# A third raw weight place and an early start of the last branch products in a hybrid decoder trunk

## The chip, the cores and the metric

The kernel runs on one core of a Trainium2 chip. Its time is the device time of one execution in microseconds (us), the median of the runs. The engines are named as in the profile: PE multiplies matrices (PEld is the loading of its stationary operand), DVE and ACT do the work on vectors, POOL does a little of it, and SP issues nearly all the transfers between HBM and the on-chip memory. SP takes its instructions in the order in which they stand in its queue, and each waits there until what it reads or overwrites is ready; every other engine's queue works in the same way. PE accumulates into PSUM, of which the kernel uses banks of 128 x 512 numbers.

## The reference

One sequence of 512 positions, 1024 channels, two layers. A layer is a half-step feed-forward block, a mixing block and a second feed-forward block, each behind a norm and ahead of another. The mixing block is where most of the change lies (cut):

```
u = _rmsnorm(h, mix_pre_g[l]);  proj = u @ w_in[l]          # q, k, v of both causal branches, f_logit, q_mem
...
z = q k^T / 8                                               # stick-breaking branch, 8 heads of 64
w = exp(log_beta + log_between)  where key < query
...
z = q k^T / 8 + c[:, None] - c[None, :]                     # forgetting branch, 8 heads of 64; c = cumsum(log_f)
p = softmax(z  where key <= query)
...
merged = (g_sb * (o_sb @ w_br_sb[l]) + g_fx * (o_fx @ w_br_fox[l]) + g_mem * (o_mem @ w_br_mem[l]))
h = h + _rmsnorm(merged @ w_out[l], mix_post_g[l])          # g_* = sigmoid(u @ w_gate[l] + b_gate[l])
```

The memory branch has 4 heads of 128 over 256 memory positions. The feed-forward blocks are SwiGLU with a hidden width of 2816.

## The kernel before, in words

**Products and weights.** Every float32 product of weights is computed as three PE products of rounded halves: high by high, high by low, low by high (`mm3`, L210, L211, L212; one "product" of 128 x 512 outputs over 1024 inputs is thus 24 matmuls). So each weight is split: a `Unit` (some 512 KB) is fetched by SP into a *raw* place (`fetch`, L254), ACT writes the high half `wh` (L180, L183), DVE subtracts it from the raw values and writes the low half `wl` (L181, L184). There are two raw places and four each for `wh` and `wl`. When a unit has been split, `loaded` gives its raw place up and calls `Q.fetch_ahead()`, which issues the next fetches in the program as long as places are free by its count. A tile also waits at run time until the reads of the one that held its place before are done. Activations are split in the same way (`split`, L180 and L181): names such as `k`, `ptf`, `pts`, `o`, `ms` in the profile.

**Mixing.** Projections give q and k for pairs of heads (products `pq`, `pk`, units `raw_q`, `raw_k`). A head then is a chain that goes through the engines:

- a stick-breaking head (`zs`, `pts`, `pvs` and `ss` in the profile) has scores on PE, sigmoids on ACT and a scan on DVE; ACT sorts the 32-bit words into two 16-bit planes (`turn_out`), SP transposes the planes in a DMA (`turn_over`, L1146, tiles `ts`), ACT puts the words together again, the result is split into `pts`, and PE multiplies it by the values (`attend`, L1170);
- a forgetting head (`zf`, `ptf`, `pvf`, `sf`) adds, for each of four row blocks, the causal mask (L1241), q·k (L1251) and a product with the cumulated forget gates (L1252; its operand `qk` is written by POOL and DVE in `fox_pre`, L1229 to L1232). DVE takes the maximum (L1254), ACT the exponential (L1256), DVE scales (L1257, L1258). Then come planes and transposes as above; DVE joins the words (`joined`, L1156), the split gives `ptf`, PE multiplies by the values (L1170), and `sf` (L1173, L1174) and its split give the branch output `o`.

While a chain is on its way, PE works on gate products (`pg`: u by `w_gate`), branch products (`pb`: `o` by `w_br`, in `merge`) and the projections of the next heads.

**What sets the order.** A planner, `Queue`, writes the program. Jobs (a product with its units) stand in a list; `step` emits the next matmuls and loads four units ahead (`AHEAD`). `weave` runs the causal heads as chains beside the jobs: a chain yields ("pe", time) or ("wait", time), the time being counted in emitted PE work (a column of a matmul counts 1/2370 us), and while it waits, jobs are emitted, up to a `limit` on the list of jobs that belongs to the head. For a forgetting head the waits are `W_FX0` = 2.0 (scores to `turn_out`), `W_FX1` = 6.0 (to `joined`) and `W_FX2` = 5.2 (to `attend`, during which the next head's scores are begun). So a larger wait in the planner means that more matmuls are written before the head's next step; how long anything really takes is not known to it. The heads come as four pairs of each kind, the forgetting pairs in the order 2, 3, 0, 1 (`FOX`).

**The end of mixing.** The gates of the forgetting branch are computed ahead and saved (`gsave`). After the last head, `run` in `merge` reloads two gates (`gb`, L1470), forms two products `pb` over the four pairs of `o`, multiplies by the gate (L1483), adds to `merged` (`mg`, L1484), and splits to `ms`; this is done four times for 8 outputs. Then come the products of `w_out` (`pwo`), which read all eight `ms`.

**Places.** Beside raw, a tag `tri` has two places. They hold split words (`ptf`, `pts`, `pt` of memory heads), the joined words of heads before the split (`pw...`), the normed memory, and hidden rows in the feed-forward blocks.

## Time and profile before

| | before |
|---|---|
| median of 3 runs | 2352.35 us (2349.74 to 2352.86) |
| the profiled execution's own time | 2350.35 us |
| its span | 2348.5 us |
| PE busy | 2311.8 us (98%), 11239 matmuls |
| DVE busy | 1801.2 us (77%) |
| ACT busy | 1600.4 us (68%) |
| transfers | 380.11 MB, mean 162 GB/s |

The span is the part of an execution that the records cover; the times of rows are microseconds from its start. A row of a group reads: line, engine, operation, output<-inputs, count, busy time, mean time of one, and behind the last bar the idle time just before them on their engine, with what ended it. In a row of the timeline the idle time of the engine before it and its releaser stand in square brackets. A row of the waits names the waiting engine with its tile, what released it, and then the idle time, the number of waits and the longest. Tiles of different layers and numbers are shown under one name in the profile (`pvf` for all forgetting heads), so a place in the program is found by its time: the mixing block of layer 0 lies near 373 to 800 us up to `w_out`, that of layer 1 near 1560 to 1965 us.

### The profile page before, as it was taken

The page shows a single profiled execution, that of the slowest core. Times are in us where ns is not written, and L with a number is a line of the kernel's source. Part 1 is how long each engine was busy: PE and PEld are TensorE (multiplying, and loading weights), DVE is VectorE, ACT ScalarE, POOL GpSimd, SP SyncE. Part 2 cuts the span into 40 slices and gives each one's busy share as a digit, 9 for nine tenths or more (in the row PEclk, how much of TensorE's full clock was granted, in tenths as well). Part 3 has the DMA queues.
Part 4 walks back from the last instruction along what each step waited for, and adds up shares of the span by engine and source line. Part 5 has one row for each costly group of instructions (what it writes and reads, how often), then busy time and mean ns, then how long its engine had stood idle before and what let it go on. Part 6 is the DMA issues. An engine that isn't in the chain of part 4 may idle for free. (4 is left out here: it accounts for less than half of the span.)

```text
span 2348.5 us, 30426 instructions
## 1 busy us (share of the span) xinstructions
PE 2311.8 (98%) x11239; PEld 1941.7 (83%) x11239; DVE 1801.2 (77%) x2291; ACT 1600.4 (68%) x2286; POOL 89.7 (4%) x182
## 2 busy tenths in 40 slices
PE   9999999999999999999999999999999999999998
PEld 7888888878788788888898888888887888888887
DVE  8877876666787688878798778766667877887785
ACT  6677466878877556775556775668788685667744
POOL 0000000000111000000000000000011100000000
PEclk9999999999999999999999999999999999999999
DMA  6667455544445654674746665555444455566744
GB/s 206 194 175 221 144 194 149 122 103 116 114 115 125 213 189 155 188 203 147 230 138 190 193 188 167 191 140 118 117 101 124 110 162 193 169 186 177 221 137 148
DMA packets 399736, 380.11 MB, mean 162 GB/s; under 512 B 180170, under 2 KB 291042, under 8 KB 399588
## 3 DMA queue, kind: packets, MB, share of 16 engines
q1 hardware_dynamic: 399492, 378.15, 55.5%
q8 instruction: 88, 1.44, 0.3%
q14 instruction: 60, 0.49, 0.1%
q0 software_dynamic: 96, 0.03, 0.0%
HBM read 319.39 MB, written 16.78 MB: 143 GB/s over the span
## 5 line engine op out<-in xcount | busy, mean ns | idle before, releaser
L210 PE MATMUL pg<-us_a,wh_wg 128*128 128x512 f32 x384 | 153.7, 400 | 8.1 <-DVE k L181 8.1
L211 PE MATMUL pg<-us_a,wh_wg 128*128 128x512 f32 x384 | 152.8, 398 | 0.0
L212 PE MATMUL pg<-us_a,wl_wg 128*128 128x512 f32 x384 | 152.5, 397 | 0.0
L181 DVE TENSOR_TENSOR wl_dc<-raw_dc,wh_dc 128x1024 fp32r<-128x1024 f32 x50 | 61.0, 1223 | 44.7 <-ACT wh_dc L180 44.7
L181 DVE TENSOR_TENSOR wl_da<-raw_da,wh_da 128x1024 fp32r<-128x1024 f32 x50 | 60.8, 1223 | 44.4 <-ACT wh_da L180 44.3
L210 PEld LDWEIGHTS pg<-us_a,wh_wg 128*128 128x128 f32 x384 | 74.2, 193 | 24.2 <-issue 8.9
L211 PE MATMUL pda<-wl_da,aha 128*128 128x512 f32 x224 | 87.7, 392 | 0.0
L211 PE MATMUL pdc<-wl_dc,ahc 128*128 128x512 f32 x224 | 87.6, 391 | 0.0
L212 PEld LDWEIGHTS pg<-us_a,wl_wg 128*128 128x128 f32 x384 | 74.1, 193 | 16.1
L212 PE MATMUL pda<-wh_da,ala 128*128 128x512 f32 x224 | 87.2, 389 | 0.0
L212 PE MATMUL pdc<-wh_dc,alc 128*128 128x512 f32 x224 | 87.2, 389 | 0.0
L210 PE MATMUL pda<-wh_da,aha 128*128 128x512 f32 x224 | 86.6, 390 | 0.5 <-ACT pda L893 0.5
L211 PEld LDWEIGHTS pg<-us_a,wh_wg 128*128 128x128 f32 x384 | 74.3, 194 | 15.4
L210 PE MATMUL pdc<-wh_dc,ahc 128*128 128x512 f32 x224 | 86.5, 389 | 0.0
L180 ACT CAST wh_dc<-raw_dc 128x1024 fp32r<-128x1024 f32 x50 | 52.3, 1049 | 47.8 <-DMA raw_dc<-in_ffn_w_down_dram 14.9
L180 ACT CAST wh_da<-raw_da 128x1024 fp32r<-128x1024 f32 x50 | 52.1, 1050 | 45.5 <-DMA raw_da<-in_ffn_w_down_dram 13.9
L184 DVE SCALAR_TENSOR_TENSOR wl_wg<-raw_wg,wh_wg 128x1024 fp32r<-128x1024 f32 x48 | 58.5, 1222 | 24.5 <-ACT wh_wg L183 24.4
L180 ACT CAST wh_uc<-raw_uc 128x1024 fp32r<-128x1024 f32 x44 | 46.4, 1053 | 34.5 <-PE pwc1g L212 8.2
L180 ACT CAST wh_ua<-raw_ua 128x1024 fp32r<-128x1024 f32 x44 | 46.2, 1052 | 30.1 <-PE pwa0g L212 8.0
L181 DVE TENSOR_TENSOR wl_uc<-raw_uc,wh_uc 128x1024 fp32r<-128x1024 f32 x44 | 53.7, 1221 | 14.9 <-ACT wh_uc L180 14.9
L181 DVE TENSOR_TENSOR wl_gc<-raw_gc,wh_gc 128x1024 fp32r<-128x1024 f32 x40 | 48.5, 1221 | 19.6 <-ACT wh_gc L180 19.6
L181 DVE TENSOR_TENSOR wl_ga<-raw_ga,wh_ga 128x1024 fp32r<-128x1024 f32 x40 | 48.5, 1221 | 19.5 <-ACT wh_ga L180 19.5
(645 smaller groups left out, 8028.3 us busy)
## 6 DMA issues: line engine op xcount, KB each, us to landing
raw_da<-in_ffn_w_down_dram SPq DMA_DIRECT2D x66, 512.0 KB, 5.0
raw_dc<-in_ffn_w_down_dram SPq DMA_DIRECT2D x66, 512.0 KB, 4.5
raw_ga<-in_ffn_w_gate_dram SPq DMA_DIRECT2D x52, 512.0 KB, 4.9
raw_ua<-in_ffn_w_up_dram SPq DMA_DIRECT2D x52, 512.0 KB, 4.4
raw_gc<-in_ffn_w_gate_dram SPq DMA_DIRECT2D x52, 512.0 KB, 4.0
raw_uc<-in_ffn_w_up_dram SPq DMA_DIRECT2D x52, 512.0 KB, 4.3
raw_wg<-in_w_gate_dram SPq DMA_DIRECT2D x48, 512.0 KB, 3.7
raw_wo<-in_w_out_dram SPq DMA_DIRECT2D x24, 512.0 KB, 3.8
```

Source lines behind the costliest of these rows:

```text
L180: both = [nc.scalar.copy(h_ap, src)]
L181: make = lambda: nc.vector.tensor_tensor(l_ap, src, h_ap.bitcast(F32), ALU.subtract)
L184: make = lambda: nc.vector.scalar_tensor_tensor(l_ap, src, scale, h_ap.bitcast(F32), ALU.mult, ALU.subtract)
L210: nc.tensor.matmul(pt, lh, rh, start=start, stop=False, skip_group_check=free)
L211: nc.tensor.matmul(pt, lh, rl, start=False, stop=False, skip_group_check=free)
L212: nc.tensor.matmul(pt, ll, rh, start=False, stop=stop, skip_group_check=free)
```

## The change

1. **Places.** `tri` has one place instead of two, a new tag `word` has one, and raw has three instead of two. What stood in the two `tri` places is now divided: split words in `tri`, joined words of causal heads in `word`; hidden rows, first weights of a block, normed memory and the words of memory heads take one of each in turn.
2. **Forgetting heads.** The four q·k products are written ahead of the four products with `qk`. The planner's wait `W_FX0` is longer by a `slack` of 4.0 for the first forgetting head of each layer, and `W_FX1` is 6.5 instead of 6.0.
3. **The last branch products.** For the first two pairs of outputs of the forgetting branch (`dp` 0 and 1) the products over three of the four pairs of `o` (`FOX[:-1]`) become a job of their own (`part`), in banks that are kept: those of `dp` 0 in the tag `mm`, those of `dp` 1 in the tag `z`. These jobs may be written beside the last causal head, whose limit now reaches to them. What is left (`rest_of`) reloads the gates, adds the product over the last pair and does the work on the vectors. The other two pairs of outputs stay as they were.

The core of the diff:

```diff
-    BUFS = {"u": 2, "v": 6, "q": 2, "k": 2, "o": 8, "tri": 2, "raw": 2, "rs": 1, "cs": 1, "wh": 4, "wl": 4, "f": 4}
+    BUFS = {"u": 2, "v": 6, "q": 2, "k": 2, "o": 8, "tri": 1, "word": 1, "raw": 3, "rs": 1, "cs": 1, "wh": 4, "wl": 4, "f": 4}
...
-                hr[i] = stile([P, FC // 2, S], ("k", "tri")[i // 2], f"hr{name}_{i}", F32)
+                hr[i] = stile([P, FC // 2, S], ("k", "k", "tri", "word")[i], f"hr{name}_{i}", F32)
...
-        word = stile([P, LAST + P], "tri", "pw" + name, F32)
+        word = stile([P, LAST + P], "word", "pw" + name, F32)
...
+        for i in reversed(range(NT)):
+            wp = max((i + 1) * P, 256)
+            nc.tensor.matmul(pzs[i][:, :wp], q[:, j, i * P:(i + 1) * P], k[:, j, :wp], start=False, stop=False,
+                             skip_group_check=True)
...
-                nc.tensor.matmul(pz[:, :wp], q[:, j, qs], k[:, j, :wp], start=False, stop=False, skip_group_check=True)
...
-        yield ("wait", W_FX0)
+        yield ("wait", W_FX0 + slack)
...
-    W_FX0, W_FX1, W_FX2 = 2.0, 6.0, 5.2
+    W_FX0, W_FX1, W_FX2 = 2.0, 6.5, 5.2
...
+            def part(done, ks, last):
+
+                if not done:
+                    done.extend(pbank(("mm", "z")[dp], f"pb{l}_{br}_{2 * dp + m}") for m in range(2))
+                for m, pt in enumerate(done):
+                    c = slice(m * P, (m + 1) * P)
+                    for k in ks:
+                        ah, al = list_act(st["o", br])(k)
+                        mm3(pt[:], ub[0].h[:, k, c], ub[0].l[:, k, c], ah, al, not last and k == ks[0], last, free=True)
+                        yield 3 * S * PE_US
+
+            def rest_of(done):
+
+                for m in range(2):
+                    gate[m] = tmp(f"gb{l}_{2 * dp + m}")
+                    nc.sync.dma_start(gate[m][:], gsave[l][2 * dp + m])
+                yield from part(done, FOX[-1:], True)
+                for m, pt in enumerate(done):
+                    add(m, pt)
...
-            if saved:
-                return lambda: Q.add(ub, run)
-            return Q.add(ub, run)
+            if not saved:
+                return Q.add(ub, run)
+            if dp < 2:
+                done = []
+                return (lambda: Q.add(ub, lambda: part(done, FOX[:-1], False))), lambda: Q.add([], lambda: rest_of(done))
+            return None, lambda: Q.add(ub, run)
...
-        for then in fox:
+        for early, _ in fox:
+            if early is not None:
+                marks["parts"] = early()
+        for _, then in fox:
             then()
...
-                                f"f{l}_{p}_{j}", lambda: pre(at, j + 1))
+                                f"f{l}_{p}_{j}", lambda: pre(at, j + 1), 0.0 if at or j else 4.0)
...
             def limit():
                 br, i, j = order[now[0]]
+                if now[0] == len(order) - 1:
+                    return marks["parts"]
                 return limits[br * NP + i][j]
```

The work on the vectors of one output moved without an edit from `run` into a function `add(m, pb)` (gate times product, add, split to `ms`).

**Three places in the order.** The planner writes another order; the number of matmuls is the same. The first place is SP's queue in the stick-breaking heads, around the fetch `raw_wb_2_1_0` (a weight of the memory branch products; `raw_q` and `raw_k` are the weights of the next pair of heads, `ts` the transposes). Before:

```order
L254 DMA raw_wg_2_1_4_4016<-in_w_gate_dram 128x4x256
L1146 DMA_TRANSPOSE ts_1_0_3_4217<-ns_1_0_3_4218 128x8x128
L1146 DMA_TRANSPOSE ts_1_0_2_4227<-ns_1_0_2_4228 128x6x128
L1146 DMA_TRANSPOSE ts_1_0_1_4239<-ns_1_0_1_4240 128x6x128
L254 DMA raw_wb_2_1_0_4172<-in_w_br_mem_dram 128x4x256
L254 DMA raw_q_0_3_4178<-in_w_in_dram 128x8x128
L254 DMA raw_k_0_3_4184<-in_w_in_dram 128x8x128
L1146 DMA_TRANSPOSE ts_1_1_3_4420<-ns_1_1_3_4421 128x8x128
```

With the change:

```order
L254 DMA raw_wg_2_1_4_4012<-in_w_gate_dram 128x4x256
L254 DMA raw_wb_2_1_0_4018<-in_w_br_mem_dram 128x4x256
L1146 DMA_TRANSPOSE ts_1_0_3_4219<-ns_1_0_3_4220 128x8x128
L1146 DMA_TRANSPOSE ts_1_0_2_4229<-ns_1_0_2_4230 128x6x128
L1146 DMA_TRANSPOSE ts_1_0_1_4241<-ns_1_0_1_4242 128x6x128
L254 DMA raw_q_0_3_4174<-in_w_in_dram 128x8x128
L254 DMA raw_k_0_3_4180<-in_w_in_dram 128x8x128
L254 DMA raw_wg_2_2_0_4186<-in_w_gate_dram 128x4x256
L1146 DMA_TRANSPOSE ts_1_1_3_4422<-ns_1_1_3_4423 128x8x128
```

`raw_wb_2_1_0` now stands ahead of the three transposes of head 1_0, and `raw_wg_2_2_0` ahead of those of head 1_1, behind which it stood before.

The second place is the first forgetting head, 2_0. On DVE its first reductions (`stf`) follow the splits of the last stick-breaking head (`pts_3_1`). Before:

```order
L181 TENSOR_TENSOR wl_k_1_3_5192<-raw_k_1_3_5125,wh_k_1_3_5191 128x1024
L181 TENSOR_TENSOR pts_3_1_5377<-pws_3_1_5371,pts_3_1_5377 128x640
L1254 TENSOR_REDUCE stf_2_0_3_5403<-zf_2_0_3_5395 128x1
L181 TENSOR_TENSOR pts_3_1_5377<-pws_3_1_5371,pts_3_1_5377 128x896
L1254 TENSOR_REDUCE stf_2_0_2_5411<-zf_2_0_2_5394 128x1
L1257 RECIPROCAL stf_2_0_3_5403<-stf_2_0_3_5403 128x1
```

With the change:

```order
L181 TENSOR_TENSOR wl_k_1_3_5194<-raw_k_1_3_5121,wh_k_1_3_5193 128x1024
L181 TENSOR_TENSOR pts_3_1_5379<-pws_3_1_5373,pts_3_1_5379 128x640
L181 TENSOR_TENSOR pts_3_1_5379<-pws_3_1_5373,pts_3_1_5379 128x896
L1257 TENSOR_REDUCE stf_2_0_3_5408<-zf_2_0_3_5397 128x1
L1257 TENSOR_REDUCE stf_2_0_2_5415<-zf_2_0_2_5396 128x1
L1257 TENSOR_REDUCE stf_2_0_1_5422<-zf_2_0_1_5395 128x1
```

Both splits of `pts_3_1` now stand ahead of the first reduction. On PE the products by the values, `pvf_2_0`, stood behind the first half of the gate product `pg_0_0`:

```order
L211 MATMUL pg_0_0_5643<-us_a_0_2946,wh_wg_0_0_0_5343 128x512
L212 MATMUL pg_0_0_5643<-us_a_0_2946,wl_wg_0_0_0_5344 128x512
L1170 MATMUL pvf_2_0_5656<-ptf_2_0_5571,v_1_1_1_4970 128x256 x4
L1170 MATMUL pvf_2_0_5656<-ptf_2_0_5571,v_1_1_0_4907 128x384 x2
L1170 MATMUL pvf_2_0_5656<-ptf_2_0_5571,v_1_1_0_4907 128x512 x2
L210 MATMUL pg_0_0_5643<-us_a_1_2947,wh_wg_0_0_4_5349 128x512
L211 MATMUL pg_0_0_5643<-us_a_1_2947,wh_wg_0_0_4_5349 128x512
```

With the change they stand in the middle of the next one, `pg_0_1`:

```order
L211 MATMUL pg_0_1_5676<-us_a_0_2948,wh_wg_0_0_0_5345 128x512
L212 MATMUL pg_0_1_5676<-us_a_0_2948,wl_wg_0_0_0_5346 128x512
L1170 MATMUL pvf_2_0_5686<-ptf_2_0_5608,v_1_1_1_4972 128x256 x4
L1170 MATMUL pvf_2_0_5686<-ptf_2_0_5608,v_1_1_0_4909 128x384 x2
L1170 MATMUL pvf_2_0_5686<-ptf_2_0_5608,v_1_1_0_4909 128x512 x2
L210 MATMUL pg_0_1_5676<-us_a_0_2948,wh_wg_0_0_0_5345 128x512
L211 MATMUL pg_0_1_5676<-us_a_0_2948,wh_wg_0_0_0_5345 128x512
```

Between the last `zf_2_0` product and the first `pvf_2_0` product stand 21 more gate matmuls than before. For the last head, 1_1, the same count grows by 3.

The third place is the last forgetting head, `pvf_1_1`, on PE. Before, it stood within the last but one gate product:

```order
L211 MATMUL pg_1_6_6925<-us_a_0_2946,wh_wg_1_3_0_6635 128x512
L212 MATMUL pg_1_6_6925<-us_a_0_2946,wl_wg_1_3_0_6636 128x512
L1170 MATMUL pvf_1_1_6938<-ptf_1_1_6886,v_1_0_1_5917 128x256 x4
L1170 MATMUL pvf_1_1_6938<-ptf_1_1_6886,v_1_0_0_5837 128x384 x2
L1170 MATMUL pvf_1_1_6938<-ptf_1_1_6886,v_1_0_0_5837 128x512 x2
L210 MATMUL pg_1_6_6925<-us_a_1_2947,wh_wg_1_3_4_6641 128x512
L211 MATMUL pg_1_6_6925<-us_a_1_2947,wh_wg_1_3_4_6641 128x512
```

With the change all gate products are ahead of it, and the branch products begin before it (`o_1_2` is the output of the first pair of heads, 2):

```order
L211 MATMUL pg_1_7_6959<-us_a_1_2949,wh_wg_1_3_4_6629 128x512
L212 MATMUL pg_1_7_6959<-us_a_1_2949,wl_wg_1_3_4_6630 128x512
L210 MATMUL pb_1_0_7015<-o_1_2_5387,wh_wb_1_0_0_6805 128x512
L211 MATMUL pb_1_0_7015<-o_1_2_5387,wh_wb_1_0_0_6805 128x512
L212 MATMUL pb_1_0_7015<-o_1_2_5387,wl_wb_1_0_0_6806 128x512
L1170 MATMUL pvf_1_1_7020<-ptf_1_1_6947,v_1_0_1_5891 128x256 x4
L1170 MATMUL pvf_1_1_7020<-ptf_1_1_6947,v_1_0_0_5789 128x384 x2
L1170 MATMUL pvf_1_1_7020<-ptf_1_1_6947,v_1_0_0_5789 128x512 x2
L210 MATMUL pb_1_0_7015<-o_1_3_5388,wh_wb_1_0_0_6805 128x512
L211 MATMUL pb_1_0_7015<-o_1_3_5388,wh_wb_1_0_0_6805 128x512
L212 MATMUL pb_1_0_7015<-o_1_3_5388,wl_wb_1_0_0_6806 128x512
L210 MATMUL pb_1_0_7015<-o_1_0_5385,wh_wb_1_0_0_6805 128x512
```

Behind these follow the other early parts up to `pb_1_3` (33 matmuls behind `pvf_1_1` in all), then the last pair's 12 matmuls for the four outputs 0 to 3, then 48 for outputs 4 to 7, then `pwo`. From the end of the first complete product, `pb_1_0`, to `pwo` stand 57 matmuls; before, it was 84.

## The prediction

> **What bounds the kernel now.** I read the page first, then the waits of PE, then the timeline around the longest waits, and last the windows for the granted clock.

> ```profile
> span 2348.5 us, 30426 instructions
> PE 2311.8 (98%) x11239; PEld 1941.7 (83%) x11239; DVE 1801.2 (77%) x2291; ACT 1600.4 (68%) x2286; POOL 89.7 (4%) x182
> ...
> PE pg L210 <- DVE k L181: 8.1, 2, 4.5
> PE pvf L1170 <- DVE ptf L181: 4.5, 6, 0.9
> PE pvf L1170 <- ACT ptf L180: 3.2, 3, 1.3
> PE pwo L211 <- DVE wl_wo L181: 2.1, 4, 0.8
> PE pvs L1170 <- DVE pts L181: 1.8, 3, 0.8
> ...
> PE zf L1252 <- POOL qk L1230: 1.0, 2, 0.5
> ```

> PE is busy for 98% and idle for 2348.5 - 2311.8 = 36.7 us; the matmuls do not change in number or size, so a gain can only come from these waits and from what follows them. What follows is the clock. In the windows below (us, then busy us of PE, PEld, DVE, ACT, POOL, then the granted clock) the five stretches right behind the longest waits run at half clock:

> ```profile
> 512.70:516.10 3.40, 3.15 (x8) 2.50 (x9) 2.39 (x5) 2.86 (x4) 1.04 (x1) 0.51 0.82 199
> 635.60:639.00 3.40, 3.40 (x10) 2.66 (x9) 3.37 (x10) 2.63 (x9) 0.96 (x2) 0.50 0.18 30
> 768.70:772.10 3.40, 3.40 (x10) 2.66 (x9) 1.28 (x3) 2.28 (x4) 0.00 (x0) 0.51 0.95 321
> 1680.10:1683.50 3.40, 3.40 (x10) 2.66 (x9) 2.02 (x3) 2.97 (x6) 0.00 (x0) 0.50 0.49 77
> 1799.60:1806.40 6.80, 5.87 (x15) 4.66 (x15) 6.71 (x16) 5.98 (x14) 2.17 (x4) 0.50 0.30 77
> ```

> The start times of matmuls of 512 columns give the price (first two rows: 3 apart at half clock; last two: 12 apart at full clock):

> ```profile
> 514.37 0.63 PE L210 MATMUL pg<-us_a,wh_wg 128*128 128x512 f32 x1
> 515.65 0.63 PE L210 MATMUL pg<-us_a,wh_wg 128*128 128x512 f32 x1
> ...
> 1961.71 0.39 PE L211 MATMUL pb<-o,wh_wb 128*128 128x512 f32 x1
> 1964.43 0.39 PE L211 MATMUL pwo<-wl_wo,ms 128*128 128x512 f32 x1
> ```

> (515.65 - 514.37) / 3 = 0.427 us against 2.72 / 12 = 0.227 us: of busy time at half clock 47% is lost. That makes 1.5, 1.6, 1.6, 1.6 and 2.8 us for the five stretches.

> **The third raw place.** The longest wait, in both layers, is at the second gate product behind keys of a stick-breaking head. Here is its chain, layer 0 and then layer 1:

> ```profile
> 479.02 1.23 DVE L181 TENSOR_TENSOR wl_k<-raw_k,wh_k 128x1024 fp32r<-128x1024 f32 x1 [3.36 <-ACT wh_k L180]
> 495.85 0.37 SPq L254 DMA_DIRECT2D raw_wb<-in_w_br_mem_dram  x1
> 499.49 1.05 ACT L180 CAST wh_wb<-raw_wb 128x1024 fp32r<-128x1024 f32 x1 [3.58 <-DMA raw_wb<-in_w_br_mem_dram]
> 500.57 1.23 DVE L181 TENSOR_TENSOR wl_wb<-raw_wb,wh_wb 128x1024 fp32r<-128x1024 f32 x1 [2.89 <-ACT wh_wb L180]
> 512.11 0.69 DVE L181 TENSOR_TENSOR k<-pk,k 64x512 fp32r<-64x512 f32 x1 [1.37 <-ACT k L180]
> 512.95 0.77 PE L210 MATMUL pg<-us_a,wh_wg 128*128 128x512 f32 x1 [4.49 <-DVE k L181]
> ...
> 1666.65 1.23 DVE L181 TENSOR_TENSOR wl_wb<-raw_wb,wh_wb 128x1024 fp32r<-128x1024 f32 x1 [2.81 <-ACT wh_wb L180]
> 1679.03 0.47 PE L210 MATMUL pg<-us_a,wh_wg 128*128 128x512 f32 x1 [3.59 <-DVE k L181]
> ...
> raw_wb<-in_w_br_mem_dram SPq DMA_DIRECT2D x8, 512.0 KB, 3.9
> ```

> The product waits for its PSUM bank, which the split of k empties; that split stands far down the queues of ACT and DVE, and both had stood still for raw_wb. With two places raw_wb could leave only at 495.85, when the unit two before it was split. With three it takes the place of k, free at 479.02 + 1.23 = 480.25, and with 3.9 us it lands near 484, long before ACT comes to it at 499.49 - 3.58 = 495.9. The order shows the fetch moved ahead of three transposes, whose words were then not yet written, so SP loses nothing there. DVE's 2.89 and 2.81 us of standing still go, and I let all behind it move up by as much: 5.7 us saved, 1.6 and 0.8 us of waiting left. A wait of 0.8 us has no half clock behind it elsewhere (below, 1778.14), one of 1.4 us has (767): so layer 1 gets 1.6 us back, layer 0 keeps its 1.5. Bounds: nothing, if k is held by something else, to 8.1 + 3.1.

> In the feed-forward parts the same place shifts fetches too. PE's waits for weights there are small (2.1 us for wl_wo is the largest group), so I put 0, between 2 us saved and 3 us lost.

> **The first forgetting head.** Its last product waits in three pieces, and the last stick-breaking head just before waits once (layer 1):

> ```profile
> 1778.14 0.91 PE L1170 MATMUL pvs<-pts,v 128*128 128x384 f32 x3 [0.81 <-DVE pts L181]
> ...
> 1797.60 0.38 PE L1170 MATMUL pvf<-ptf,v 128*128 128x256 f32 x1 [1.30 <-ACT ptf L180]
> 1798.86 0.80 PE L1170 MATMUL pvf<-ptf,v 128*128 128x256 f32 x4 [0.88 <-DVE ptf L181]
> 1800.58 1.54 PE L1170 MATMUL pvf<-ptf,v 128*128 128x384 f32 x3 [0.93 <-DVE ptf L181]
> ```

> That is 3.1 us; of the 7.7 us of all pvf waits the last heads (next part) hold 1.6, so layer 0 has 3.0. The order puts 21 more matmuls before this product: 21 x 0.227 = 4.8 us of cover against 3.1, while the list of ACT and DVE up to ptf stays as it was. Saved: 6.1 us, and 1.6 + 2.8 = 4.4 of half clock. The slack only moves work that is done anyway; its price is that less is left for later heads, which comes below. In DVE's order the second split of pts now stands before the first reduction of zf; a DVE pass of 512 columns is 0.69 us (the k row), so I take 0.6 of each wait of 0.8: 1.2 us.

> The q·k products of all row blocks now go ahead of the products that wait for POOL's qk: some 0.4 us of cover against two waits of 0.5. I take 0.8 of the 1.0.

> **The last forgetting head** waits in layer 0, and 0.2 us in layer 1:

> ```profile
> 766.82 0.44 PE L1170 MATMUL pvf<-ptf,v 128*128 128x384 f32 x1 [0.70 <-ACT ptf L180]
> 767.94 0.91 PE L1170 MATMUL pvf<-ptf,v 128*128 128x384 f32 x3 [0.69 <-DVE ptf L181]
> ...
> 1932.85 0.90 PE L1170 MATMUL pvf<-ptf,v 128*128 128x384 f32 x3 [0.21 <-DVE ptf L181]
> ```

> It gets 3 more matmuls of cover (0.7 us), and three weight splits that DVE had in this stretch come earlier, at 1.2 us each. I take all 1.6 us and the 1.6 of half clock.

> Saved in all: 5.7 + 1.6 + 6.1 + 4.4 + 1.2 + 0.8 + 1.6 + 1.6 = 23.0 us.

> **What is late next.** First the second forgetting head. ACT and DVE are behind there, and PE's wait was what let them catch up:

> ```profile
> 1816.28 1.46 DVE L181 TENSOR_TENSOR ptf<-pwf,ptf 128x896 fp32r<-128x896 f32 x1
> 1821.04 1.46 PE L1170 MATMUL pvf<-ptf,v 128*128 128x256 f32 x8
> ...
> 1800.00:1821.00 21.00, 20.42 (x90) 17.01 (x91) 18.99 (x40) 18.71 (x37) 4.38 (x8) 0.85 0.45 107
> ```

> The slack was 1821.04 - (1816.28 + 1.46) = 3.3 us, with PE slowed by 2.8 us of half clock. Without that PE comes 1 to 3 us earlier, and the order puts one or two more splits (1.2 us each) on DVE before ptf, which at 18.99 of 21 us has little room. I take a wait of 1.0 us in each layer and one stretch of half clock, 3.6 us; bounds 0 and 2 x (2.5 + 1.6) = 8.2.

> Second, the end of mixing. The four products begun early now end together, and 57 matmuls stand from the end of the first to w_out, where 84 stood. DVE's run from the first gate to the last ms is

> ```profile
> 1947.37 0.69 DVE L1483 TENSOR_TENSOR gb<-gb,pb 128x512 f32<-128x512 f32 x1 [1.79 <-PE pb L212]
> 1969.65 0.68 DVE L181 TENSOR_TENSOR ms<-mg,ms 128x512 fp32r<-128x512 f32 x1
> ```

> 23.0 us, against (57 + 42) x 0.227 = 22.5 until PE asks for the eighth ms. I take 0.5 us a layer, between 0 and 2. The reloads of gates (gb) have 8 us of other products before them. Costs: 4.6 us.

> **The sum** against the profiled execution's own time of 2350.35 (span 2348.5 and 1.85 around it): 2350.35 - 23.0 + 4.6 = 2332. That execution lay 2.0 us under the median of the runs, so I say 2333.

> [...]

> **Rivals.** (1) The wait moves: the heads after the first are held by ACT and DVE, and the second and third give back 6.1 + 4.4. For it: 90% busy DVE. Against it: from the third head on the trace shows no waits for ptf until the last. 2333 + 10.5 - 3.6 = 2340. (2) The third place does nothing for k, because the fetch waits in SP's line or k is held elsewhere: 7.3 us stay, 2340. Against it: the row at 479.02. (3) Slower: SP's queue is one line, and in nearly all 32 causal heads a fetch that waits for a split now stands ahead of transposes that used to go first. If that holds the words back by a split, 1.23 us, beyond the head's slack, PE pays in each such head; from 15 heads on the gain is gone, and with 20 and two stretches of half clock it is 2333 + 24.6 + 3.2 = 2361. Against it: the places asked for are mostly free by then, as at 480.25. [...]

> **How the numbers follow.** Forecast 0.57, (1) 0.20, (2) 0.08, (4) 0.06, (3) 0.09. All gains with no cost, 2 us more in the feed-forward parts and layer 0's clock give 2324; upper bounds of both costs, 3 us lost there and half of case (1) give 2346. The range is 2325 to 2346. A measurement of this kernel can tell 0.2% (4.7 us) from nothing. Faster by more is the forecast, (2), (4) and most of (1): 0.87; within it 0.05; slower 0.08.

> **What would show it.** Right: no pg wait on k over 2 us, raw_wb landed before its cast, no pvf wait at the first and last head, at most two stretches of half clock in mixing, pieces of about 1 us at the second head. Wrong: waits of pvf at later heads, transposes issued late behind raw fetches, pwo waiting for ms, or new waits for weights in the feed-forward parts.

## The result, and the profile after

The changed kernel takes 2359.56 us (median of 6 runs, 2356.44 to 2363.74) against 2352.61 us for the kernel before (6 runs, 2349.74 to 2354.28). The ratio is 1.0032 with a 95% interval of 1.0019 to 1.0046: slower by a third of a percent, where 2333 and faster was forecast.

The first lines of the changed kernel's page, and the longest waits of PE:

```profile
span 2358.2 us, 30419 instructions
PE 2312.8 (98%) x11239; PEld 1944.9 (82%) x11239; DVE 1807.8 (77%) x2291; ACT 1604.2 (68%) x2286; POOL 90.8 (4%) x182
...
PE pwc1g L210 <- ACT pwc1g L759: 5.2, 1, 5.2
PE pvf L1170 <- DVE ptf L181: 4.5, 4, 1.5
PE pwc0g L210 <- ACT pwc0g L759: 3.8, 1, 3.8
PE pwa0g L210 <- ACT pwa0g L759: 3.6, 1, 3.6
PE pwa1g L210 <- ACT pwa1g L759: 3.4, 1, 3.4
PE pk L210 <- DVE ga L205: 3.0, 2, 2.2
PE pwa0g L210 <- ACT sa L787: 2.6, 1, 2.6
...
PE pg L210 <- DVE k L181: 1.7, 1, 1.7
```

The two longest waits of before, `pg` on `k` behind the stick-breaking keys, are gone; the 1.7 us that this row still shows is one wait at another place, at 723.68 us among the forgetting heads. The `pvf` row is no longer the first forgetting head but the second (below). New are waits on a line that the prediction never named: L759, in the feed-forward blocks. Which part of the program lost shows best in the windows of the five parts: feed-forward; mixing with `w_out`; the two feed-forward blocks between; mixing with `w_out`; feed-forward. The first number behind the stretch is its length in us, then come the busy times of PE, PEld, DVE, ACT and POOL. Before:

```profile
0.00:373.30 373.30, 368.58 (x1776) 306.83 (x1777) 300.40 (x349) 244.04 (x329) 6.38 (x14) 1.00 0.62 189
373.30:847.20 473.90, 461.29 (x2302) 389.42 (x2301) 337.78 (x538) 351.50 (x561) 41.11 (x83) 0.99 0.51 133
847.20:1541.10 693.90, 691.64 (x3314) 579.99 (x3313) 560.52 (x596) 446.21 (x576) 2.17 (x3) 1.00 0.59 181
1541.10:2011.00 469.90, 459.95 (x2301) 388.99 (x2300) 338.07 (x538) 350.62 (x561) 40.02 (x82) 0.99 0.51 134
2011.00:2348.50 337.50, 330.37 (x1553) 276.51 (x1551) 264.41 (x274) 208.07 (x259) 0.00 (x0) 1.00 0.56 172
```

With the change:

```profile
0.00:381.50 381.50, 371.80 (x1776) 309.33 (x1777) 304.55 (x351) 246.56 (x331) 6.37 (x14) 0.99 0.62 188
381.50:844.30 462.80, 456.29 (x2302) 387.43 (x2301) 336.69 (x536) 350.84 (x561) 41.51 (x83) 1.00 0.53 136
844.30:1550.30 706.00, 695.78 (x3313) 583.50 (x3312) 565.01 (x597) 448.58 (x576) 2.19 (x3) 0.99 0.60 178
1550.30:2013.60 463.30, 456.68 (x2301) 387.09 (x2300) 336.84 (x537) 350.79 (x562) 40.73 (x82) 1.00 0.52 136
2013.60:2358.20 344.60, 332.24 (x1553) 277.60 (x1551) 264.75 (x272) 207.46 (x257) 0.00 (x0) 0.99 0.57 165
```

Mixing gained 11.1 + 6.6 = 17.7 us, where 18.4 had been forecast. The feed-forward blocks lost 8.2 + 12.1 + 7.1 = 27.4 us, where 0 had been put. The two leave a loss of 9.7 us, which is the difference of the spans. So the question is why the feed-forward blocks are slower.

ACT's timeline ahead of the longest new wait, with the waiting product of PE behind it:

```profile
2124.61 1.98 ACT L180 CAST wh_gc<-raw_gc 128x1024 fp32r<-128x1024 f32 x2
2127.84 1.33 ACT L820 COPY hrc<-trc1u 128x1024 uint16<-128x1024 uint16 x1 [1.24 <-DMA trc1u<-thc1u]
2129.04 1.03 ACT L812 COPY thc1u<-sc 128x1024 uint16<-128x1024 uint16 x1
2129.98 1.04 ACT L180 CAST wh_gc<-tgc 128x1024 fp32r<-128x1024 f32 x1
2130.92 0.57 ACT L759 COPY pwc1g<-pwc1g 128x512 f32<-128x512 f32 x1
...
2131.55 0.80 PE L210 MATMUL pwc1g<-wh_gc,us_b 128*128 128x512 f32 x1 [5.22 <-ACT pwc1g L759]
```

And ACT at the same place before:

```profile
2120.46 1.36 ACT L820 COPY hrc<-trc1u 128x1024 uint16<-128x1024 uint16 x1 [1.36 <-DMA trc1u<-thc1u]
2121.68 1.04 ACT L180 CAST wh_gc<-raw_gc 128x1024 fp32r<-128x1024 f32 x1
2122.62 0.58 ACT L759 COPY pwc1g<-pwc1g 128x512 f32<-128x512 f32 x1
```

L759 copies the first sums of the second hidden chunk into another PSUM bank, on which PE goes on adding; PE cannot begin the product without it. Before, the copy stood right behind the two casts of the product's weights. Now, behind the same two casts, a copy of transposed words (L820, which waits 1.24 us for its transpose and takes 1.33), a sort into planes (L812, 1.03) and a cast of a later weight (L180, 1.04) stand ahead of it. The rows of ACT's order at that place, before:

```
L180 CAST wh_gc_1_1_0_18531<-raw_gc_1_1_0_18354 128x1024
L820 COPY hrc_1_18299<-trc1u_5_18511 128x2x4x128
L180 CAST wh_gc_1_1_2_18535<-raw_gc_1_1_2_18440 128x1024
L759 COPY pwc1g_1_0_18628<-pwc1g_0_0_18495 128x512
L812 COPY thc1u_6_0_18597<-sc_0_10_18260 128x1024
L759 COPY pwc1g_1_1_18629<-pwc1g_0_1_18496 128x512
L180 CAST wh_gc_1_3_0_18570<-tgc_1_0_18350 128x1024
```

With the change:

```
L180 CAST wh_gc_1_1_0_18533<-raw_gc_1_1_0_18318 128x1024
L180 CAST wh_gc_1_1_2_18539<-raw_gc_1_1_2_18356 128x1024
L820 COPY hrc_1_18299<-trc1u_5_18514 128x2x4x128
L812 COPY thc1u_6_0_18597<-sc_0_10_18260 128x1024
L180 CAST wh_gc_1_3_0_18570<-tgc_1_0_18310 128x1024
L759 COPY pwc1g_1_0_18636<-pwc1g_0_0_18497 128x512
```

The same exchange stands in all four feed-forward blocks. No line of the diff moves these instructions (it does change the place of some rows that L820 writes; the first experiment keeps that edit and clears it). The framework's scheduler orders each engine's queue at build time, and with a third place for raw weights it ordered ACT otherwise.

### The profile page after: what moved, and what is told of

Same layout as the page of the kernel before. It is cut to its first block, busy times and chain, and to the rows that moved or that the text cites. A ratio compares the mean times of both kernels' runs of the same rounds, so it can differ in the third digit from the quotient of the medians.

```text
span 2358.2 us, 30419 instructions
## 1 busy us (share of the span) xinstructions
PE 2312.8 (98%) x11239; PEld 1944.9 (82%) x11239; DVE 1807.8 (77%) x2291; ACT 1604.2 (68%) x2286; POOL 90.8 (4%) x182
## 5 line engine op out<-in xcount | busy, mean ns | idle before, releaser
L210 PE MATMUL pg<-us_a,wh_wg 128*128 128x512 f32 x384 | 150.1, 391 | 1.7 <-DVE k L181 1.7
L212 PE MATMUL pg<-us_a,wl_wg 128*128 128x512 f32 x384 | 149.6, 390 | 0.0
L211 PE MATMUL pg<-us_a,wh_wg 128*128 128x512 f32 x384 | 149.5, 389 | 0.0
L181 DVE TENSOR_TENSOR wl_dc<-raw_dc,wh_dc 128x1024 fp32r<-128x1024 f32 x50 | 61.2, 1224 | 39.5 <-ACT wh_dc L180 39.5
L181 DVE TENSOR_TENSOR wl_da<-raw_da,wh_da 128x1024 fp32r<-128x1024 f32 x50 | 61.2, 1223 | 38.8 <-ACT wh_da L180 38.8
L211 PE MATMUL pdc<-wl_dc,ahc 128*128 128x512 f32 x224 | 87.6, 391 | 0.0
L211 PE MATMUL pda<-wl_da,aha 128*128 128x512 f32 x224 | 87.6, 391 | 0.0
L212 PE MATMUL pdc<-wh_dc,alc 128*128 128x512 f32 x224 | 87.2, 389 | 0.0
L212 PE MATMUL pda<-wh_da,ala 128*128 128x512 f32 x224 | 87.2, 389 | 0.0
L210 PE MATMUL pda<-wh_da,aha 128*128 128x512 f32 x224 | 86.6, 390 | 0.2 <-ACT pda L893 0.2
L210 PE MATMUL pdc<-wh_dc,ahc 128*128 128x512 f32 x224 | 86.5, 389 | 0.0
L210 PEld LDWEIGHTS pg<-us_a,wh_wg 128*128 128x128 f32 x384 | 72.1, 188 | 16.5 <-issue 2.1
L212 PEld LDWEIGHTS pg<-us_a,wl_wg 128*128 128x128 f32 x384 | 72.1, 188 | 15.4
L211 PEld LDWEIGHTS pg<-us_a,wh_wg 128*128 128x128 f32 x384 | 72.2, 188 | 14.6
L180 ACT CAST wh_uc<-raw_uc 128x1024 fp32r<-128x1024 f32 x44 | 46.3, 1052 | 42.7 <-PE pwc0g L212 11.4
L180 ACT CAST wh_dc<-raw_dc 128x1024 fp32r<-128x1024 f32 x50 | 52.6, 1051 | 33.3 <-PE pdc L212 23.3
L180 ACT CAST wh_ua<-raw_ua 128x1024 fp32r<-128x1024 f32 x44 | 46.2, 1052 | 42.5 <-PE pwa0g L212 13.0
L180 ACT CAST wh_da<-raw_da 128x1024 fp32r<-128x1024 f32 x50 | 52.6, 1051 | 32.2 <-PE pda L212 23.9
L1156 ACT COPY pws<-ts 128x1024 uint16<-128x1024 uint16 (+1 forms) x64 | 54.7, 915 | 15.4 <-DMA ts<-ns 15.2
L181 DVE TENSOR_TENSOR wl_ga<-raw_ga,wh_ga 128x1024 fp32r<-128x1024 f32 x40 | 48.6, 1222 | 16.7 <-ACT wh_ga L180 16.6
L181 DVE TENSOR_TENSOR wl_gc<-raw_gc,wh_gc 128x1024 fp32r<-128x1024 f32 x40 | 48.7, 1222 | 15.3 <-ACT wh_gc L180 15.0
## 6 DMA issues: line engine op xcount, KB each, us to landing
raw_da<-in_ffn_w_down_dram SPq DMA_DIRECT2D x66, 512.0 KB, 4.6
raw_dc<-in_ffn_w_down_dram SPq DMA_DIRECT2D x66, 512.0 KB, 4.5
raw_ga<-in_ffn_w_gate_dram SPq DMA_DIRECT2D x52, 512.0 KB, 4.7
raw_ua<-in_ffn_w_up_dram SPq DMA_DIRECT2D x52, 512.0 KB, 4.1
raw_gc<-in_ffn_w_gate_dram SPq DMA_DIRECT2D x52, 512.0 KB, 4.4
raw_uc<-in_ffn_w_up_dram SPq DMA_DIRECT2D x52, 512.0 KB, 4.3
raw_wg<-in_w_gate_dram SPq DMA_DIRECT2D x48, 512.0 KB, 4.0
raw_wo<-in_w_out_dram SPq DMA_DIRECT2D x24, 512.0 KB, 4.5
```

Source lines behind the costliest of these rows:

```text
L180: both = [nc.scalar.copy(h_ap, src)]
L181: make = lambda: nc.vector.tensor_tensor(l_ap, src, h_ap.bitcast(F32), ALU.subtract)
L210: nc.tensor.matmul(pt, lh, rh, start=start, stop=False, skip_group_check=free)
L211: nc.tensor.matmul(pt, lh, rl, start=False, stop=False, skip_group_check=free)
L212: nc.tensor.matmul(pt, ll, rh, start=False, stop=stop, skip_group_check=free)
L1156: copy(block_words(word, i), over[:, :, c:c + i + 1])
```

## The experiments

**Does the third place cost it, and is it the order it gives?** Four kernels on one chip (before: 2348.57 us there). The first lets the third place be used in mixing only (`RINGS["third"]` is set to 1 at the start of a mixing block's heads and to 0 behind them):

```diff
-"word": 1, "raw": 3,
+"word": 1, "raw": 2, "third": 1,
-    RINGS = {"raw": BUFS["raw"], "o": 0, "v": 0}
+    RINGS = {"raw": BUFS["raw"], "third": 0, "o": 0, "v": 0}
...
                         if un.place in RINGS and self.fetched[un.place] >= RINGS[un.place]:
-                            return
+                            if un.place != "raw" or self.fetched["third"] >= RINGS["third"]:
+                                return
+                            un.place = "third"
```

> The changed kernel, but the third raw place is to be had only while the mixing blocks run; in the feed-forward blocks there are two, and the order of every engine there is that of the kernel before. Theory A (the third place costs the 27.3 us that the feed-forward blocks gained in time, through the order it gives there): they take 361, 718 and 322.5 us again, mixing keeps its 17.6 us of gain, and the time is 2352.6 - 17.6 = 2335, faster than both. Theory B (the loss comes from the divided tri places, from where the tiles lie or from a later start, not from the third place): the feed-forward blocks stay near 369, 730 and 329 us, and the time stays near 2359.

Measured: 2328.29 us, ratio 0.9914 (0.9898 to 0.9931). The feed-forward parts in its profile:

```profile
0.00:372.40 372.40, 368.08 (x1775) 307.10 (x1776) 300.98 (x349) 244.02 (x329) 6.38 (x14) 1.00 0.62 190
...
834.30:1525.90 691.60, 690.65 (x3313) 580.48 (x3313) 561.28 (x596) 445.90 (x576) 2.18 (x3) 1.00 0.59 182
...
1986.00:2324.10 338.10, 330.37 (x1553) 276.57 (x1551) 263.46 (x274) 207.91 (x259) 0.00 (x0) 1.00 0.55 170
```

They take 372.4, 691.6 and 338.1 us, against 373.3, 693.9 and 337.5 before (the expectation had cut the span into parts at other places). The loss is gone, with the divided `tri` places kept. Theory B falls. This version beats both kernels; its mixing, too, is 4.1 us shorter than with the change.

The second has two raw places and the rest of the change:

```diff
-"word": 1, "raw": 3,
+"word": 1, "raw": 2,
```

> The changed kernel with two raw places instead of three and nothing else. Theory A: the feed-forward blocks are as before, and mixing loses what the third place gave there, the waits of 4.5 and 3.6 us for the bank of k and their half clock: about 2335 + 7 to 10 = 2342 to 2345. Theory B: about 2367.

Measured: 2340.17 us, 0.9962 (0.9947 to 0.9977). In mixing alone the third place is worth 2340.17 - 2328.29 = 11.9 us. The waits on `k` are back in its profile:

```profile
PE pg L210 <- DVE k L181: 9.7, 3, 4.5
```

The third is the reverse, the kernel before with the places of the change and nothing else:

> The kernel before with the third raw place and the divided tri places, without the changes to the forgetting heads and the branch products. Theory A: the feed-forward loss of 27 us in full, in mixing only the 7 us of the stick-breaking wait back: 2352.6 + 27 - 7 = 2372. Theory B with the loss in the head changes or in the later start: 2345.

Measured: 2360.54 us, 1.0052 (1.0037 to 1.0067), 12 us slower than before. In its profile the feed-forward parts take 381.4, 705.7 and 345.0 us (loss 27.4), and the four waits on L759 are there (3.8, 3.8, 3.1 and 4.5 us). Mixing gains 16 us there, more than the 7 that were expected of it, so the time is between the two numbers; the places alone carry the loss in full, without the other edits.

The fourth keeps all three places everywhere and only holds L820 behind L759 on ACT:

```diff
-                    nc.scalar.copy(st["c", ci, up, 1][e][:], st["c", ci, up, 0][e][:])
+                    st["moved"] = nc.scalar.copy(st["c", ci, up, 1][e][:], st["c", ci, up, 0][e][:])
...
-                    with tc.issue_after(st["second"].cast.ins) if last else nullcontext():
+                    behind = st["second"].cast if last else st.get("moved")
+                    with tc.issue_after(behind.ins) if behind is not None else nullcontext():
                         nc.scalar.copy(dst_, src_)
```

> The changed kernel with all three places everywhere; on ACT the copies of turned words (L820) are held behind the copies of a product's first sums (L759) that are ahead of them in the program. Only some 30 rows of ACT's order move, those around the new waits. Theory A1 (the order on ACT is the cause: a copy that waits for a transpose stands ahead of the copy that PE waits for): the waits of 3.6, 3.8, 3.4 and 5.2 us and their half clock (about 1.6 each, 2.8 at the third) go, 16 + 7.6 = 23.6 us: 2359.6 - 23.6 = 2336. Theory A2 (the transposes are late because fetches stand ahead of them on SP, and ACT is late whatever its order): the wait only moves to the next product, and the time stays above 2350.

Measured: 2340.16 us, 0.9963 (0.9948 to 0.9978). Its longest waits:

```profile
PE pvf L1171 <- DVE ptf L181: 4.6, 4, 1.5
PE mt L1069 <- DVE mraw L1062: 2.5, 1, 2.5
PE pda L210 <- ACT pda L894: 2.4, 2, 1.9
...
PE pwa0g L210 <- ACT sa L787: 1.9, 1, 1.9
```

All four waits on L759 are gone, though the transposes are little earlier: L820 still waits 42.6 us in all for them, against 47.5 with the change and 34.8 before. So the order on ACT, and not the lateness of the transposes alone, made those waits (theory A1, not A2). But by the two ratios (0.9963, and 1.0032 with the change) the kernel is 16 us faster than the changed one, not 23.6, and it is 11.9 us slower than the first experiment. Its feed-forward parts take 378.0, 698.4 and 338.1 us, together 17.6 us less than with the change. So this one exchange made some 60% of the 27.4 us, and 9.8 us are left. In these parts PE still waits for the copy of sums L787 (1.9 us, at 62 us; 2.6 with the change), for L894 (1.9, where the same copy cost 0.2 with the change) and, for another reason than a copy on ACT, for `mraw` on DVE (2.5; 1.8 with the change, 0.6 in all before). The rest is not taken apart.

**What are the other edits worth?** Four kernels on the base of the first experiment (before: 2350.91 us there). The base itself was 0.9914 above and 0.9899 in a second measurement below, so a difference of under some 4 us from a base that was measured on another chip shows nothing.

The planner's waits as before:

```diff
-    W_FX0, W_FX1, W_FX2 = 2.0, 6.5, 5.2
+    W_FX0, W_FX1, W_FX2 = 2.0, 6.0, 5.2
...
-                                f"f{l}_{p}_{j}", lambda: pre(at, j + 1), 0.0 if at or j else 4.0)
+                                f"f{l}_{p}_{j}", lambda: pre(at, j + 1), 0.0)
```

> On top of the kernel with the third place in mixing alone (20.3 us faster than before): the planner's waits as before, no slack for the first forgetting head and 6.0 instead of 6.5. Theory A (the cover ahead of the first head is worth what the prediction gave it, 6.1 us of wait and 4.4 of clock, and its price is the wait at the second head, 4.6 us of wait and 3.2 of clock in the profile): the first heads wait again for some 3 us each, the second heads do not wait, and the time is 10.5 - 7.8 = 3 us longer. Theory B (the first head's wait is gone because ACT and DVE are earlier with the third place, and the waits did nothing): no wait at either head, 5 to 8 us shorter.

Measured: 2335.21 us, 0.9935 (0.9921 to 0.995). The first head waits again:

```profile
624.22 0.38 PE L1172 MATMUL pvf<-ptf,v 128*128 128x256 f32 x1 [2.15 <-ACT ptf L180]
625.49 1.33 PE L1172 MATMUL pvf<-ptf,v 128*128 128x256 f32 x4 [0.89 <-DVE ptf L181]
```

There is no wait at the second head of layer 0, and one of 0.5 us in layer 1. Theory A: the cover is worth its price, by 5 us or more. The loss is larger than the 3 us expected; a wait for `qk` (2.2 us) and waits of the last head (1.4 and 1.3 us), which the expectation did not have, came too.

The early branch products undone (`dp < 2` made `dp < 0`, and the last head's limit as before):

> The same base, with the last branch products as before, none of them beside the last causal head. Theory A: the last head of layer 0 waits 1.4 us again and has half clock behind it, layer 1 waits 0.2, the end of mixing is as it was: 3 to 4 us longer. Theory B (with the third place the splits ahead of the last head are early anyway): within 1 us.

Measured: 2336.19 us, 0.9941 (0.9926 to 0.9956), 6 us or more behind the base. Neither theory holds: the loss is larger than both said, and the wait is not at `pvf` but behind it: in this order the branch products follow the last head's `pvf` at once, without gate products between, and soon ask for that head's output. Half clock follows (layer 0: products of 512 columns start 0.43 us apart from 774.20 us on, against 0.23 at 771.42; in layer 1 the same wait is 1.3 us):

```profile
771.08 0.50 PE L210 MATMUL pb<-o,wh_wb 128*128 128x512 f32 x1 [2.69 <-DVE sf L1176]
```

q·k next to the product with `qk`, as before:

> The same base, each q.k product next to its product with qk, as before. Theory A: two waits of 0.5 us for POOL come back, 1 us longer, within what can be told. Theory B (the wait for qk is hidden by the other edits): no difference.

Measured: 2325.77 us, 0.9895 (0.9879 to 0.9912). No wait for POOL came back. Its time even lies below the base's, so both were measured again on one chip:

> The third place in mixing alone, once more and on one chip with the next kernel, in five rounds: 0.991 of the time before again if the gain of 20 us holds.

> The same with each q.k product next to its product with qk. It was 0.9895 of before against 0.9914 for the base, the intervals overlapping. Theory A (the reordering of q.k saves the two waits for POOL): 1 us longer than the base. Theory B (it does nothing, since no wait for POOL came back in the profile): the two agree within 0.1%. Theory C (the reordering costs, because the first maximum on DVE can begin only after all four q.k products): shorter than the base by 3 to 5 us again.

Measured: base 2326.68 us, 0.9899 (0.9882 to 0.9915); q·k as before 2325.17 us, 0.9894 (0.9879 to 0.9909). The two agree: the reordering of q·k does nothing here. So the kernel with q·k as before may stand for the base among the four that ran on one chip. There the two undone edits above cost 9.4 and 10.4 us against it, and the added slack below 8.8.

A slack of 3.0 for the second forgetting head as well (`0.0 if at else (4.0, 3.0)[j]`):

> The same base with a slack of 3.0 for the second forgetting head too (some 14 matmuls of cover). Theory A (the wait at the second head is a want of cover at that place alone, since ACT and DVE catch up by the third): its 2.3 us and the 1.6 us of half clock go in both layers, 7.8 us shorter, 2320. Theory B (cover only moves the wait on, ACT and DVE are behind by a fixed amount): the third head waits 1 to 2 us with half clock behind it, within 2 us of the base.

Measured: 2334.59 us, 0.9936 (0.9922 to 0.9951), 5 us or more slower than the base. Second head and last head of layer 0:

```profile
650.08 0.38 PE L1172 MATMUL pvf<-ptf,v 128*128 128x256 f32 x1 [0.50 <-ACT ptf L180]
650.94 0.80 PE L1172 MATMUL pvf<-ptf,v 128*128 128x256 f32 x4 [0.48 <-DVE ptf L181]
652.54 1.41 PE L1172 MATMUL pvf<-ptf,v 128*128 128x384 f32 x3 [0.81 <-DVE ptf L181]
...
771.16 0.38 PE L1172 MATMUL pvf<-ptf,v 128*128 128x256 f32 x1 [2.38 <-ACT ptf L180]
772.02 0.89 PE L1172 MATMUL pvf<-ptf,v 128*128 128x256 f32 x3 [0.48 <-DVE ptf L181]
773.55 0.69 PE L1172 MATMUL pvf<-ptf,v 128*128 128x384 f32 x1 [0.65 <-ACT ptf L180]
774.69 1.54 PE L1172 MATMUL pvf<-ptf,v 128*128 128x384 f32 x3 [0.46 <-DVE ptf L181]
```

The second head's 2.3 us (1.48 and 0.81 in the base's profile) shrank to 1.8 only, and the last head waits 4.0 us, where the base did not wait at all. Theory A falls. Theory B had the direction right, but the size too small and the place wrong: not the third head, but the last one pays. A likely reason, which no run here tests alone: the number of products that can stand beside the heads is given, and a longer wait at one head takes them from another.

## Why the prediction was wrong, point by point

**The step that failed** is the last paragraph on the third place: "In the feed-forward parts the same place shifts fetches too. PE's waits for weights there are small [...], so I put 0, between 2 us saved and 3 us lost." It cost 27.4 us. The bound was taken from the waits for weights, as if an earlier fetch could change nothing but when a weight is there. (Even so the row was misread: `wl_wo` belongs to `w_out`, in mixing. The largest wait for a weight in the feed-forward parts was 0.5 us.) What changed was the order of ACT's queue, and through it the copy (L759) that PE waits for. The trace of before had the sign, in one of the four places:

```profile
PE pwa0g L210 <- ACT pwa0g L759: 1.0, 1, 1.0
```

The copy was already just late there, so what was put ahead of it could be paid in full.

**Mixing** came out as forecast in sum, 17.7 against 18.4, and that is partly luck. The sum gave the third place 7.3 us and all other edits 11.1, as if the two did not touch each other. In the profiles the places alone give mixing 16.2 us (third experiment), the other edits without the third place 8.1 (second), and both together 17.7: they overlap.

- The third place for `raw_wb`: forecast 7.3 us, the run without it shows 11.9. The fetch leaves and lands early, as said, and the waits on `k` at the stick-breaking heads are gone altogether, not by 2.9 us each. With the change its cast comes at 501.69, and mixing began 8.2 us later, so at 493.5 by the times of before, against 499.49: it moved up by 6.0 us. The split of k that frees the bank moved up by 5.3 (515.04 - 8.2 = 506.8, against 512.11), more than the whole wait of 4.5. The term was mis-sized: what DVE stood still for at one instruction was less than what the chain through ACT gained.

```profile
485.17 0.37 SPq L254 DMA_DIRECT2D raw_wb<-in_w_br_mem_dram  x1
501.69 1.05 ACT L180 CAST wh_wb<-raw_wb 128x1024 fp32r<-128x1024 f32 x1
515.04 0.69 DVE L181 TENSOR_TENSOR k<-pk,k 64x512 fp32r<-64x512 f32 x1 [1.40 <-ACT k L180]
```

- The first forgetting head: right. No wait, no half clock in either layer (granted clock 1.00 from 137.8 to 660.0 us and from 1305.2 to 1875.2); undoing the planner's waits brings the waits back (2.15 and 0.89 us in the rows of that run), and behind them four products of 256 columns take 1.33 us, against 0.80 at full clock in the rows below.
- The second head as the next to be late: right in place, short in size. Forecast 2.0 us and one stretch of half clock, measured 4.5 and one (granted clock 0.50 from 660.03 to 663.45 us; the rows below, layer 0 and layer 1). With that clock's 1.6 us it is 6.1, against 3.6 forecast and an upper bound of 8.2.

```profile
657.54 0.80 PE L1170 MATMUL pvf<-ptf,v 128*128 128x256 f32 x4 [1.38 <-DVE ptf L181]
659.15 0.90 PE L1170 MATMUL pvf<-ptf,v 128*128 128x384 f32 x3 [0.81 <-DVE ptf L181]
...
1827.32 0.80 PE L1170 MATMUL pvf<-ptf,v 128*128 128x256 f32 x4 [1.47 <-DVE ptf L181]
1828.93 0.91 PE L1170 MATMUL pvf<-ptf,v 128*128 128x384 f32 x3 [0.80 <-DVE ptf L181]
...
1874.85 0.53 PE L210 MATMUL pk<-us_a,wh_k 128*128 128x512 f32 x1 [2.18 <-DVE ga L205]
```

- Missed: `pk` waits for a bank that the gates' addition (`ga`, L205) empties, 2.2 us with half clock behind it in layer 1 (last row; granted clock 0.50 from 1875.18 to 1878.58 us), 0.8 in layer 0; and `pg` waits 1.7 us for k in layer 0, at 723.68.
- The last stick-breaking head (`pvs`): 1.2 us forecast, 0.7 measured (1.8 us of waits before, 1.1 now). The last forgetting head: right, with the half clock (granted 1.00 from 663.45 to 960.40 us, where before had 0.50 from 768.74 to 772.15). The end of mixing: the prediction took 1.0 us lost; there is no wait for `ms` at all, and `w_out` lost its own waits for weights (47.0 and 47.5 us before, 45.3 and 45.3 now).
- q·k: the waits for POOL went as forecast, but not by this edit.
- A slip of 1 us: the sum gives 2332, and the 2.0 us to the median would make it 2334, not 2333. It changes nothing here.

**The rivals.** (1), waits at the second and third heads: in part, at the second only. (2), the third place does nothing for `k`: no. (3), a line of SP holding back the heads' transposes: not seen at any head, since no later `pvf` waits. Its time, 2361, is close to the measured one by accident; the slower side came from another engine and another block. (4), no clock lost behind the small waits that are left: no run shows that this holds for all of them, and the wait of 2.18 us above has 3.4 us of half clock behind it.

The chance of 0.08 for slower, made of one mishap in mixing, was too small because the feed-forward blocks, whose places the diff changes too, had been given no case of their own.

**What stays open:** why the scheduler ordered ACT so. That it did is in the order, and that undoing one exchange brings back 16 us is measured; its reasons are not visible here. The other 9.8 us of the loss go with the third place too, since they are gone without it, but the waits that make them up were not tested one by one.

## What to carry to other kernels

In this kernel the size of a pool was an input to the order of other engines, in every block that uses the pool. When a change adds or divides a place, compare the order of all engines in all blocks, look for instructions that PE waits for (copies that empty or fill a PSUM bank) and see what now stands ahead of them. Give a resource only to the stage whose wait it removes: with the third place in mixing alone the same change is 0.9 to 1.0% faster than before.

## What the runs showed of the hardware that was not expected

```profile
656.62:660.03 3.41, 1.68 (x9) 1.34 (x10) 3.41 (x6) 0.30 (x1) 0.32 (x1) 1.00 0.48 154
660.03:663.45 3.42, 3.42 (x19) 3.42 (x18) 3.34 (x14) 3.37 (x11) 0.00 (x0) 0.50 0.00 0
1823.98:1827.40 3.42, 1.96 (x17) 1.75 (x15) 3.42 (x7) 2.00 (x3) 0.00 (x0) 1.00 0.49 144
1827.40:1830.81 3.41, 2.61 (x17) 2.25 (x18) 3.36 (x8) 1.30 (x5) 0.32 (x1) 1.00 0.43 148
```

The idle times are 3.41 - 1.68 = 1.73 us, in two pieces, and in layer 1 3.42 - 1.96 = 1.46 and 3.41 - 2.61 = 0.80 us. This fits with why waits of the same length had half clock or not: the second head's 2.2 us in layer 0 fell mostly into one stretch, its 2.3 us in layer 1 were divided between two. Between 1.6 and 1.9 us the sum alone does not decide either: before, 1.82 us at 632.2 had half clock behind it, and with the change 1.82 us at 1496.3 and 1.69 us at 721.5 had none.
